# Attention probabilities transposed on VectorE in 32x32 squares, with the squares exchanged through DRAM, in a two-layer diffusion backbone

## The chip, the cores and the metric

The kernel runs on one core of one Trainium2 chip. The metric is the device time of one execution in microseconds, lower is better. Four engines do the work: TensorE (PE in the profile, with its weight loads as PEld), VectorE (DVE), ScalarE (ACT) and GpSimd (POOL). SyncE (SP) issues nearly all DMAs; ACT issues the few of the rotary swap.

## The reference

Two layers work on a latent stream of 1024 tokens with 1024 channels. The first is windowed attention with 16 query heads over 4 key/value heads of 128 channels, the second a gated convolution module. Only the attention is touched. Each block of 128 queries sees its own block of keys, the block before, the block after and 256 context keys, in one softmax with a learned sink:

```
s_win = einsum('bqhgd,bkhd->bhgqk', qblk, kw) * scale
s_win = where(mask, s_win, -inf)
s_ctx = einsum('bqhgd,bchd->bhgqc', qblk, kc) * scale
p_ctx, p_win = sink_softmax(sink_l, s_ctx, s_win)
o = einsum('bhgqc,bchd->bqhgd', p_ctx, vc) + einsum('bhgqk,bkhd->bqhgd', p_win, vw)
```

`y = (o * silu(z)) @ w_out`, and the layer adds `gate * y` to its input. The scores leave TensorE with queries on the partitions; the product with the values wants the probabilities with keys on the partitions. So every block of probabilities, 128 queries by 512 or 640 keys, must be transposed.

## The kernel before, in words

Each f32 operand is split into a high and a low part, and a product is three matmuls (high by high, high by low, low by high). The kernel has a first part (modulation, the projections of the first heads), the attention, the output projection, and the convolution layer.

The attention is a loop over 128 steps (line 1280): 16 heads, and in each head 8 blocks of 128 queries. I write a step as (head, block). TensorE's instructions stand in the order of the program; those of the other engines are put in order by a scheduler that works ahead of the run. What step (h, b) puts on TensorE, in this order:

- `scores` (line 1083) of the **next** step: six matmuls into one of two PSUM buffers `pss`. Behind them on the other engines: DVE adds the mask and takes the maximum (`p_page<-pss`, here "the reduce"), ACT takes the exponential and its sum, DVE the reciprocal, POOL scales by it ("the scale"). The result is `p_page`.
- `fill(12)` (line 1070): twelve matmuls of the q and z projections of the next head, into `psg`.
- `pv` (line 1153) if it is due. `pv(h, half)` multiplies four blocks of probabilities by values and context values: 18 matmuls that read `pthi` and `ptlo`. It is put into a queue behind block 3 or 7 and so stands in the step after that. `pv(5, 0)` stands in step (5, 4), `pv(5, 1)` in step (6, 0). I call the stretch between two `pv` a half. Behind every second head `pv_shared` does the two edges between the halves.
- `transposes` (line 1119) of the step's own block: 4 or 5 transposes of 128x128 on TensorE into a `pss` buffer, then ACT copies them to `pthi` (the high part, "hi"), and DVE subtracts to get `ptlo` ("lo").

At the end of every fourth head there is a longer step ("regroup", line 1308), in which the whole k and v projections of the next group run on TensorE.

`pthi` and `ptlo` have 22 places of 128 columns. The places of a block are used again by the block four steps later, so hi of (h, 4) can't be written until `pv(h, 0)` has read them.

Beside this, DVE does one step of a long sum per loop step (`ada_rest`, line 665: "ada" below, 0.48 us each, its input loaded by SP one step ahead); it is held behind the lo of the softmax (`after`, line 660). `low_parts` (line 724) makes the low parts of the output weights on ACT ("lhi") and POOL, and SP stores them. SBUF is handed out as 45 pages of 4 KB per partition in turn.

Of the kernel before, what the change touches and what calls it, by code (L numbers as in the profile page):

```python
# [14 lines left out]
P = 128  # L15
# [15 lines left out]
TB = T // P  # L31
# [63 lines left out]
def backbone_kernel(  # L95
# [987 lines left out]
    def scores(h, qb):  # L1083
        g = h // 4
        q = qt[h]
        kk = kvt[g]
        c = kk[2]
        k0, k1 = max(qb - 1, 0), min(qb + 1, TB - 1)
        nw = (k1 - k0 + 1) * P
        s = ps_s()  # L1090
        w0 = 512 - nw
        qsl = slice(qb * P, qb * P + P)
        ksl = slice(k0 * P, k0 * P + nw)
        for n, (a, b) in enumerate(((0, 0), (0, 1), (1, 0))):
            PE.matmul(s[:, w0:512], q[a][:, qsl], kk[b][:, ksl], start=n == 0, stop=n == 2)
            PE.matmul(s[:, 512:768], q[a][:, qsl], c[:, b], start=n == 0, stop=n == 2)
        p = pg.alloc(F32, [1024], "p")
        sc8 = small([P, 3], name="sc", bufs=6)
        nmx, l0, ri = (sc8[:, i:i + 1] for i in range(3))
        w = nw + CT  # L1100

        act(p[:, w:w + 1], nsink[:, h:h + 1], AF.Copy)
        sc = dict(scale=-SCALE, scalar=nsink[:, h:h + 1], op0=ALU.add, op1=ALU.min, accum_out=nmx)
        if qb == TB - 1:
            V.tensor_tensor_reduce(
                out=p[:, 0:w].rearrange("p (a b) -> p a b", a=2),
                in0=s[:, w0:768].rearrange("p (a b) -> p a b", a=2),
                in1=mask.rearrange("p (a b) -> p a b", a=2)[:, :, 0:256],
                **sc)
        else:  # L1110
            V.tensor_tensor_reduce(out=p[:, 0:w], in0=s[:, w0:768], in1=mask[:, 640 - w:640], **sc)
        act(p[:, 0:w + 1], p[:, 0:w + 1], AF.Exp, bias=nmx, scale=-1.0, accum_out=l0)
        V.reciprocal(ri, l0)
        anchor_p[:] = [G.tensor_scalar(out=p[:, 0:w], in0=p[:, 0:w], scalar1=ri, scalar2=1.0, op0=ALU.mult, op1=ALU.mult)]
        ptile[(h, qb)] = p
        if qb == TB - 1:
            pg.free(*qt.pop(h))

    def transposes(h, qb):
        p = ptile.pop((h, qb))  # L1120
        k0, k1 = max(qb - 1, 0), min(qb + 1, TB - 1)
        nb = k1 - k0 + 1
        tb = ps_s()
        ql = qb % 4
        for kb in range(k1, k0 - 1, -1):
            at = 2 - 2 * (kb - qb)
            PE.transpose(tb[:, at * P:(at + 1) * P], p[:, (kb - k0) * P:(kb - k0 + 1) * P], ident)
        for i in range(2):
            at = 1 + 2 * i
            PE.transpose(tb[:, at * P:(at + 1) * P], p[:, (nb + i) * P:(nb + i + 1) * P], ident)  # L1130
        pg.free(p)
        tv = tb[:, 0:640].rearrange("p (a b) -> p a b", b=P)
        a0, a1 = int(qb == TB - 1), 4 if qb == 0 else 5
        runs = [(a0, a1, slice(ql + 4 * a0, ql + 4 * a1 - 3, 4))]
        if h % 2 == 0 and qb == 3:
            runs = [(1, 5, slice(7, 20, 4)), (0, 1, slice(20, 21))]
        elif h % 2 == 0 and qb == 4:
            runs = [(0, 4, slice(0, 13, 4)), (4, 5, slice(21, 22))]
        for r0, r1, bs in runs:
            anchor_a[:] = [act(pthi[:, bs], tv[:, r0:r1], AF.Copy)]  # L1140
        for r0, r1, bs in runs:
            anchor[:] = [split_lo(V, ptlo[:, bs], tv[:, r0:r1], pthi[:, bs])]

    shared = []

    def pv_mm(o, work):
        for n, (a, b, ps_, os_) in enumerate(work):
            last = n == len(work) - 1
            PE.matmul(o[:, os_], a, pthi[:, ps_], start=n == 0, stop=False)
            PE.matmul(o[:, os_], a, ptlo[:, ps_], start=False, stop=False)  # L1150
            PE.matmul(o[:, os_], b, pthi[:, ps_], start=False, stop=last)

    def pv(h, half):
        if half == 2:
            return pv_shared(h)
        c, vh, vl = kvt[h // 4][2:5]
        o = ps_o(0)
        q0 = half * 4
        work = [(*(c[:, n, i * P:i * P + P] for n in (2, 3)), slice(4 + 8 * i, 8 + 8 * i), slice(0, 512)) for i in range(2)]
        for kb in range(q0, q0 + 4):  # L1160
            qa, qz = max(kb - 1, q0), min(kb + 1, q0 + 3)
            b0 = qa - q0 + 8 * (qa - kb + 1)
            work.append((vh[:, kb], vl[:, kb], slice(b0, b0 + 9 * (qz - qa) + 1, 9), slice((qa - q0) * P, (qz - q0 + 1) * P)))
        pv_mm(o, work)
        sl = slice(half * 512, half * 512 + 512)
        if h % 2 == 0 and half == 0:
            shared[:] = [pg.alloc(F32, [1024], "ozs")]
        part = shared[0]
        oz = hp.alloc(F32, None, "oz")
        own, edge = (slice(128, 512), slice(0, 128)) if half else (slice(0, 384), slice(384, 512))  # L1170
        zv = zt[h][:, sl]
        e0 = 256 * half + 128 * (1 - h % 2)
        stt(oz[:, 0:512], o, 0.5, zv, ALU.mult, ALU.mult)
        V.tensor_copy(part[:, e0:e0 + 128], oz[:, edge])
        SY.dma_start(out=ozd[h, :, sl][:, own], in_=oz[:, own])
        hp.free(oz)
        if half:
            act(part[:, 768 - 256 * (h % 2):1024 - 256 * (h % 2)], zt[h][:, 384:640], AF.Copy)
            pg.free(zt.pop(h))

    def pv_shared(h):

        vh, vl = kvt[h // 4][3:5]

        o = ps_o(0)
        pv_mm(o[:, 0:256], [(vh[:, 4], vl[:, 4], slice(3, 21, 17), slice(0, 256))])
        pv_mm(o[:, 256:512], [(vh[:, 3], vl[:, 3], slice(16, 22, 5), slice(0, 256))])
        part = shared.pop()
        oz = hp.alloc(F32, None, "oz")
        ov, sv, pv_ = (t[:, 0:512].rearrange("p (q e n) -> p e q n", q=2, e=2) for t in (o, oz, part))  # L1190
        zv = part[:, 512:1024].rearrange("p (e q n) -> p e q n", q=2, e=2)
        for e in range(2):
            stt(sv[:, e], ov[:, e], 0.5, zv[:, e], ALU.mult, ALU.mult)
        tt(V, oz[:, 0:512], oz[:, 0:512], part[:, 0:512], ALU.add)
        for e in range(2):
            SY.dma_start(out=ozd[h - e, :, 384:640].rearrange("p (q n) -> p q n", q=2), in_=sv[:, e])
        hp.free(oz)
        pg.free(part)
        if h % 4 == 3:
            pg.free(vh, vl)  # L1200
# [79 lines left out]
    for i, (h, qb) in enumerate(steps):  # L1280
        if qb == 0:
            for n in (() if h % 4 == 3 else (h + 1,) if h % 4 or not h else (h, h + 1)):
                enqueue(("z", n))
                if n + 1 < NH:
                    enqueue(("q", n + 1))
        if (h, qb) == (NH - 1, EARLY_FROM - 2):
            run(lows)
        if h == NH - 1 and EARLY_FROM - 2 <= qb < EARLY_FROM:
            next(projA)
        if (h, qb) == (NH - 1, EARLY_FROM):  # L1290
            next(projA)
            fillq.append((("wo", 0), early_proj()))
        nxt = steps[i + 1] if i + 1 < len(steps) else None
        regroup = nxt and nxt[1] == 0 and nxt[0] % 4 == 0
        if nxt and nxt[1] == 0:
            fill(1000, ("q", h + 1))
        if nxt and not regroup:
            scores(*nxt)
        if not regroup:
            n = 15 if h and h % 4 == 0 and qb < 4 else FILL  # L1300
            if h // 4 in vlate and h:
                fill(3)
                n -= 3
                vlate.pop(h // 4)()
            fill(n)
        if pvq:
            pv(*pvq.popleft())
        if regroup:
            g = nxt[0] // 4
            old = kvt[g - 1]  # L1310
            run(job(("k", g)))
            transposes(h, qb)
            run(job(("v", g)))
            pv(h, 1)
            pg.free(*old[:3])
            scores(*nxt)
            continue
        transposes(h, qb)
        if lstate[0] == "open" or h and (h % 4 < 3 or qb < LOWS):
            lstate[0] = next(lows, "shut")  # L1320
        else:
            store()
        if qb % 4 == 3:
            pvq.append((h, qb // 4))
        if qb == 1 and h and h % 2 == 0:
            pvq.append((h - 1, 2))
        for _ in range(2 if qb == 1 or qb == 6 and h % 2 else 1):
            if next(adag, None):
                break
# [646 lines left out]
```

## Time and profile before

| | |
|---|---|
| runs of the kernel before | 1686.21, 1686.81, 1686.99 us; median 1686.81 |
| span of the profiled execution | 1684.8 us, first to last instruction |
| outside the span | 2.0 us, median less span (the profiled execution's own whole time isn't listed) |
| PE busy | 1675.0 us, 99% |
| DVE, ACT, POOL busy | 1116.1, 878.8, 871.0 us |
| DMA | 244.55 MB, 145 GB/s over the span |
| granted TensorE clock | 0.999 |

The attention loop lies between about 75 and 805 us. A busy time says in how much of the span an instruction of that engine was under way. Matmuls overlap, so the pace of TensorE is read from the starts of its instructions, not from their durations. The order in which instructions stand on DVE and SP decides what waits behind what, since each engine runs its own list in order.

### The profile page before, as it was taken

The page shows a single profiled execution, that of the slowest core. Times are in us where ns is not written, and L with a number is a line of the kernel's source. Part 1 is how long each engine was busy: PE and PEld are TensorE (multiplying, and loading weights), DVE is VectorE, ACT ScalarE, POOL GpSimd, SP SyncE. Part 2 cuts the span into 40 slices and gives each one's busy share as a digit, 9 for nine tenths or more (in the row PEclk, how much of TensorE's full clock was granted, in tenths as well). Part 3 has the DMA queues.
Part 4 walks back from the last instruction along what each step waited for, and adds up shares of the span by engine and source line. Part 5 has one row for each costly group of instructions (what it writes and reads, how often), then busy time and mean ns, then how long its engine had stood idle before and what let it go on. Part 6 is the DMA issues. An engine that isn't in the chain of part 4 may idle for free.

```text
span 1684.8 us, 23963 instructions
## 1 busy us (share of the span) xinstructions
PE 1675.0 (99%) x8436; PEld 1413.9 (84%) x8436; DVE 1116.1 (66%) x2131; ACT 878.8 (52%) x1555; POOL 871.0 (52%) x722
## 2 busy tenths in 40 slices
PE   9999999999999999999999999999999999999998
PEld 6888888888888888888888888888888888888886
DVE  5765654566356644566324289999999999868732
ACT  5745543555355543556334365555665654566741
POOL 0256653666366663653001267999898888130400
PEclk9999999999999999999999999999999999999999
DMA  9424443454244443447976522020211202387881
GB/s 387 150 85 153 134 121 95 153 153 141 84 152 144 143 135 98 135 135 251 320 233 228 213 94 91 11 72 17 75 51 51 82 33 80 130 276 241 310 298 50
DMA packets 114776, 244.55 MB, mean 145 GB/s; under 512 B 11626, under 2 KB 36514, under 8 KB 114656
## 3 DMA queue, kind: packets, MB, share of 16 engines
q1 hardware_dynamic: 108576, 233.06, 40.9%
q10 hardware_dynamic: 6080, 9.97, 2.4%
q8 instruction: 66, 1.08, 0.3%
q14 instruction: 54, 0.44, 0.1%
HBM read 190.80 MB, written 41.69 MB: 138 GB/s over the span
## 4 chain that ended last, share of the span: by engine, by line
PE 98%; DVE 0%; DMA 0%; ACT 0%; POOL 0%; issue 0%; ACTq 0%; POOLq 0%
PE psg L89 51%; PE pss L89 26%; PE pso L89 22%; DMA rope_half<-rope_half 0%; POOL rope_half L89 0%; DVE x_page L89 0%; ACT p_page L89 0%; DVE wlo_page L89 0%; ACT pthi L89 0%; ACT rope_half L89 0%; ACT whi_page L89 0%; DVE hf_page L89 0%; DVE hl_page L89 0%; ACT qh_page L89 0%; ACT lhi_page L89 0%
## 5 line engine op out<-in xcount | busy, mean ns | idle before, releaser
L89 POOL TENSOR_TENSOR odd_half<-odd_half,prod_half 128x513 f32<-128x513 f32 (+2 forms) x252 | 314.7, 1257 | 22.6 <-ACT prod_half L89 9.4
L89 POOL TENSOR_TENSOR wlo_page<-wraw_page,whi_page 128x512 fp32r<-128x512 f32 (+1 forms) x104 | 173.0, 1680 | 186.7 <-DVE ql_page L89 72.0
L89 PE MATMUL psg<-hh_page,whi_page 128*128 128x512 f32 x600 | 236.3, 394 | 0.0
L89 PE MATMUL psg<-hl_page,whi_page 128*128 128x512 f32 x600 | 234.4, 391 | 0.0
L89 PE MATMUL psg<-hh_page,wlo_page 128*128 128x512 f32 x600 | 234.0, 390 | 0.0
L89 ACT ACTIVATE prod_half<-ubuf,dww 128x513 f32<-128x513 f32 (+2 forms) x252 | 165.6, 675 | 116.9 <-POOL odd_half L89 113.0
L89 PE MATMUL psg<-h2h_page,whi_page 128*128 128x512 f32 x464 | 181.9, 392 | 0.0
L89 PE MATMUL psg<-h2h_page,wlo_page 128*128 128x512 f32 x464 | 180.6, 389 | 0.0
L89 PE MATMUL psg<-h2l_page,whi_page 128*128 128x512 f32 x464 | 180.6, 389 | 0.0
L89 POOL TENSOR_SCALAR p_page<-p_page,sc 128x640 f32<-128x640 f32 (+1 forms) x128 | 99.6, 779 | 149.5 <-DVE sc L89 131.8
L89 DVE SCALAR_TENSOR_TENSOR pss<-ubuf,dww,pss 128x512 f32<-128x512 f32 (+3 forms) x270 | 172.4, 670 | 0.1
L89 DVE SCALAR_TENSOR_TENSOR pss<-ubuf,wsum,pss 128x512 f32<-128x512 f32 (+3 forms) x270 | 171.7, 671 | 0.2
L89 ACT ACTIVATE p_page<-p_page,sc 128x641 f32<-128x641 f32 (+1 forms) x128 | 102.9, 804 | 98.3 <-DVE sc L89 95.9
L89 ACT ACTIVATE pthi<-pss 128x512 fp32r<-128x512 f32 (+2 forms) x144 | 87.3, 618 | 109.7 <-PE pss L89 99.8
L89 DVE TENSOR_TENSOR ptlo<-pss,pthi 128x512 fp32r<-128x512 f32 (+2 forms) x144 | 101.8, 716 | 61.2 <-ACT pthi L89 59.9
L89 PEld LDWEIGHTS psg<-hh_page,wlo_page 128*128 128x128 f32 x600 | 112.7, 188 | 24.3
L89 PEld LDWEIGHTS psg<-hh_page,whi_page 128*128 128x128 f32 x600 | 112.8, 188 | 19.2 <-ACT hh_page L89 0.3
L89 PEld LDWEIGHTS psg<-hl_page,whi_page 128*128 128x128 f32 x600 | 112.8, 188 | 18.4
L89 ACT ACTIVATE whi_page<-wraw_page 128x1024 fp32r<-128x1024 f32 x88 | 92.6, 1052 | 49.8 <-PE psg L89 21.1
L89 PE MATMUL pso<-h2h_page,whi_page 128*128 128x512 f32 x304 | 118.3, 389 | 0.0
L89 PE MATMUL pso<-h2h_page,wlo_page 128*128 128x512 f32 x304 | 118.3, 389 | 0.0
L89 PE MATMUL pso<-h2l_page,whi_page 128*128 128x512 f32 x304 | 118.3, 389 | 0.0
(262 smaller groups left out, 3992.4 us busy)
## 6 DMA issues: line engine op xcount, KB each, us to landing
wraw_page<-in_k_wconv_dram SPq DMA_DIRECT2D x48, 512.0 KB, 3.3
wraw_page<-in_k_win_dram SPq DMA_DIRECT2D x40, 512.0 KB, 3.6
wo_page<-in_attn_w_out_dram SPq DMA_DIRECT2D x32, 512.0 KB, 6.2
wol_page<-wolA SPq DMA_DIRECT2D x32, 512.0 KB, 8.3
wo_page<-in_conv_w_out_dram SPq DMA_DIRECT2D x32, 512.0 KB, 6.7
wol_page<-wolC SPq DMA_DIRECT2D x32, 512.0 KB, 6.2
rope_half<-rope_half ACTq DMA_DIRECT2D x76, 128.0 KB, 2.4
araw_page<-in_k_ada_dram SPq DMA_DIRECT2D x16, 512.0 KB, 10.1
```

The lines of the kernel that those rows point to most:

```text
L89: r = f(*a, **k)
```

## The change

The four or five transposes on TensorE go. In `scores`, behind the scale, DVE now transposes the block in squares of 32x32 into a new page (`psq_page`, below "T"): within each strip of 32 partitions the squares are turned, but a square stays in its strip. SP stores that page to one of four DRAM buffers (`squares`). `land`, at the start of the block's own step, issues four loads on SP, one for each strip of 32 partitions, which fetch the squares that belong there into another page (`pt_page`). `split_p` then makes hi on ACT and lo on DVE from that page in SBUF, where before both read PSUM. The order of the places in `pthi` and `ptlo` changes with it, and `pv_mm` takes them as access patterns made by hand; the matmuls are the same in number and size.

```diff
@@ scores
-        ptile[(h, qb)] = p
+        nt = w // P
+        sq = pg.alloc(F32, [1024], "psq")
+        V.transpose(out=sq[:, 0:w].rearrange("p (b t j) -> p t b j", b=4, t=nt),
+                    in_=p[:, 0:w].rearrange("p (t b j) -> p t b j", t=nt, b=4))
+        pg.free(p)
+        z = squares[(h * TB + qb) % len(squares)]
+        SY.dma_start(out=z[:, 0:w], in_=sq[:, 0:w])
+        pg.free(sq)
...
-    def transposes(h, qb):
+    squares = [dr.tile([P, 640], F32, tag=f"psq{i}", name=f"psq{i}") for i in range(4)]
+
+    def land(h, qb):
+
+        nt = 4 if qb in (0, TB - 1) else 5
+        z = squares[(h * TB + qb) % len(squares)]
+        p = ptile[(h, qb)] = pg.alloc(F32, [1024], "pt")
+        for b in range(4):
+            SY.dma_start(out=p[32 * b:32 * b + 32, 0:nt * P].rearrange("p (a x) -> p a x", a=4),
+                         in_=z[:, b * nt * 32:(b + 1) * nt * 32].rearrange("(a p) x -> p a x", p=32))
...
+    def split_p(h, qb):
...
-            PE.transpose(tb[:, at * P:(at + 1) * P], p[:, (kb - k0) * P:(kb - k0 + 1) * P], ident)
...
-            PE.transpose(tb[:, at * P:(at + 1) * P], p[:, (nb + i) * P:(nb + i + 1) * P], ident)
+        pv_ = p[:, 0:nt * P].rearrange("p (a t j) -> p t a j", a=4, t=nt)
...
-            anchor_a[:] = [act(pthi[:, bs], tv[:, r0:r1], AF.Copy)]
+            anchor_a[:] = [act(slots(pthi, b0, r1 - r0), pv_[:, r0:r1], AF.Copy)]
...
-            anchor[:] = [split_lo(V, ptlo[:, bs], tv[:, r0:r1], pthi[:, bs])]
+            anchor[:] = [split_lo(V, slots(ptlo, b0, r1 - r0), pv_[:, r0:r1], slots(pthi, b0, r1 - r0))]
...
@@ the loop over steps
+        land(h, qb)
         if nxt and not regroup:
             scores(*nxt)
...
-        transposes(h, qb)
+        split_p(h, qb)
```

How this stands on DVE in head 5, at blocks 4 to 6. Before, the rows from the reciprocal of block (5, 5) on; `ptlo_76<-pss_248` is lo of (5, 4), `ptlo_76<-pss_252` lo of (5, 5), and the `ISA` row is the reduce of (5, 6):

```order
L89 RECIPROCAL sc_246_3382<-sc_246_3382 128x1
L89 TENSOR_TENSOR rope_half_75_3458<-psg_243_3349,cos_page_78_560 128x512
L89 SCALAR_TENSOR_TENSOR oz_half_72_3419<-pso_247_3400,zs_page_226_3156 128x512
L89 COPY ozs_page_218_3012<-oz_half_72_3419 128x128
L89 TENSOR_TENSOR ptlo_76<-pss_248_3423,pthi_75 128x5x128
L89 ISA p_page_239_3442,sc_250_3443<-pss_249_3435,mask_page_82_597,nsink_72 128x640
L89 ISA sc_250_3443 128x1
L89 RECIPROCAL sc_250_3443<-sc_250_3443 128x1
L89 COPY mod1_604<-pso_69_945 128x2
L89 TENSOR_TENSOR ptlo_76<-pss_252_3480,pthi_75 128x5x128
```

Now, the same place; `pt_page_321`, `326` and `330` are blocks (5, 3), (5, 4) and (5, 5), `psq_page_328` is T of (5, 5), and `oz_half_72` reads the result of `pv(5, 0)`:

```order
L89 TENSOR_TENSOR ptlo_76<-pt_page_321_3451,pthi_75 128x5x128
L89 SCALAR_TENSOR_TENSOR pso_69_952<-wsum_raw_606,cs_131,pso_69_952 128x256
L89 STREAM_TRANSPOSE psq_page_328_3515<-p_page_327_3508 128x5x4x32
L89 COPY mask_page_82_597<-pso_69_952 128x256
L89 TENSOR_TENSOR ptlo_76<-pt_page_326_3496,pthi_75 128x5x128
L89 SCALAR_TENSOR_TENSOR oz_half_72_3549<-pso_203_3530,zs_page_307_3272 128x512
L89 ISA p_page_331_3571,sc_205_3572<-pss_204_3564,mask_page_82_597,nsink_72 128x640
L89 ISA sc_205_3572 128x1
L89 COPY ozs_page_293_3122<-oz_half_72_3549 128x128
L89 TENSOR_TENSOR ptlo_76<-pt_page_330_3559,pthi_75 128x5x128
L89 COPY mod1_604<-pso_69_952 128x2
L89 RECIPROCAL sc_205_3572<-sc_205_3572 128x1
```

What moved: lo of (5, 3), which stood ahead of the rows shown, now stands ahead of T of (5, 5). Lo of (5, 5) now stands ahead of the reciprocal of (5, 6), so the softmax of (5, 6) can't go on until (5, 5) has come back from DRAM.

The same place on SP. Before:

```order
L89 DMA dww_raw_605<-in_ada_w_dram 128x256
L89 DMA wsum_raw_606<-in_ada_w_dram 128x256
L89 DMA wolA_607<-low_page_232_3286 128x1024
L89 DMA wraw_page_242_3454<-in_k_win_dram 128x1024
L89 DMA ozd_601<-oz_half_72_3419 128x384
L89 DMA low_page_246_3583<-in_attn_w_out_dram 128x2x512
```

Now; a row `psq..` is the store of a block, `pt_page.. x4` its four loads, for blocks (5, 3), (5, 4) and (5, 5):

```order
L89 DMA psq3_613<-psq_page_320_3430 128x640
L89 DMA dww_raw_605<-in_ada_w_dram 128x256
L89 DMA psq0_610<-psq_page_323_3470 128x640
L89 DMA pt_page_321_3451<-psq3_613 32x4x160 x4
L89 DMA pt_page_326_3496<-psq0_610 32x4x160 x4
L89 DMA wsum_raw_606<-in_ada_w_dram 128x256
L89 DMA psq1_611<-psq_page_328_3515 128x640
L89 DMA wolA_607<-low_page_317_3404 128x1024
L89 DMA pt_page_330_3559<-psq1_611 32x4x160 x4
```

What moved: SP has five more DMAs for each step, and the loads of (5, 3) stand behind the store of (5, 4), which waits for that block's T.

More of the change, by code (lines that the diff above doesn't have):

```diff
@@ L1116, in scores @@
+        pg.free(sq)
         if qb == TB - 1:
             pg.free(*qt.pop(h))
-    def transposes(h, qb):
-        p = ptile.pop((h, qb))
[L1121 to L1126, printed above, removed]
-            PE.transpose(tb[:, at * P:(at + 1) * P], p[:, (kb - k0) * P:(kb - k0 + 1) * P], ident)
-        for i in range(2):
-            at = 1 + 2 * i
-            PE.transpose(tb[:, at * P:(at + 1) * P], p[:, (nb + i) * P:(nb + i + 1) * P], ident)
-        pg.free(p)
[L1132 to L1139, printed above, removed]
-            anchor_a[:] = [act(pthi[:, bs], tv[:, r0:r1], AF.Copy)]
-        for r0, r1, bs in runs:
-            anchor[:] = [split_lo(V, ptlo[:, bs], tv[:, r0:r1], pthi[:, bs])]
@@ new lines, in backbone_kernel, with slots @@
+    squares = [dr.tile([P, 640], F32, tag=f"psq{i}", name=f"psq{i}") for i in range(4)]
[6 more added lines that the diff above has]
+                         in_=z[:, b * nt * 32:(b + 1) * nt * 32].rearrange("(a p) x -> p a x", p=32))
+    def slots(t, b0, n):
+        return t[:, b0:b0 + 4 * n - 3:4].rearrange("p t (a j) -> p t a j", a=4)
@@ new lines, in split_p @@
+    def split_p(h, qb):
+        p = ptile.pop((h, qb))
+        ql, a0 = qb % 4, int(qb == 0)
+        nt = 4 if qb in (0, TB - 1) else 5
+        pv_ = p[:, 0:nt * P].rearrange("p (a t j) -> p t a j", a=4, t=nt)
+        if qb == 0:
+            runs = [(0, 4, 4)]
+        elif qb == TB - 1:
+            runs = [(0, 2, ql), (2, 4, ql + 12)]
+        elif h % 2 == 0 and qb == 3:
+            runs = [(0, 2, ql), (3, 5, ql + 12), (2, 3, 20)]
+        elif h % 2 == 0 and qb == 4:
+            runs = [(1, 5, ql + 4), (0, 1, 21)]
+        else:
+            runs = [(0, 5, ql)]
+        for r0, r1, b0 in runs:
+            anchor_a[:] = [act(slots(pthi, b0, r1 - r0), pv_[:, r0:r1], AF.Copy)]
+        for r0, r1, b0 in runs:
+            anchor[:] = [split_lo(V, slots(ptlo, b0, r1 - r0), pv_[:, r0:r1], slots(pthi, b0, r1 - r0))]
+        pg.free(p)
@@ L1144, in backbone_kernel, with pthi_lo @@
     shared = []
+    def pthi_lo(b0, step, n):
+        return [bass.AP(t.tensor, t.offset + b0 * P, [t.ap[0], (step * P, n), (1, P)])
+                for t in (pthi[:, 0:22].rearrange("p b n -> p (b n)"), ptlo[:, 0:22].rearrange("p b n -> p (b n)"))]
     def pv_mm(o, work):
@@ L1148, in pv_mm @@
             last = n == len(work) - 1
-            PE.matmul(o[:, os_], a, pthi[:, ps_], start=n == 0, stop=False)
-            PE.matmul(o[:, os_], a, ptlo[:, ps_], start=False, stop=False)
-            PE.matmul(o[:, os_], b, pthi[:, ps_], start=False, stop=last)
+            ph, pl = ps_
+            PE.matmul(o[:, os_], a, ph, start=n == 0, stop=False)
+            PE.matmul(o[:, os_], a, pl, start=False, stop=False)
+            PE.matmul(o[:, os_], b, ph, start=False, stop=last)
     def pv(h, half):
@@ L1158, in pv @@
         q0 = half * 4
-        work = [(*(c[:, n, i * P:i * P + P] for n in (2, 3)), slice(4 + 8 * i, 8 + 8 * i), slice(0, 512)) for i in range(2)]
+        work = [(*(c[:, n, i * P:i * P + P] for n in (2, 3)), pthi_lo(12 + 4 * i, 1, 4), slice(0, 512)) for i in range(2)]
         for kb in range(q0, q0 + 4):
             qa, qz = max(kb - 1, q0), min(kb + 1, q0 + 3)
-            b0 = qa - q0 + 8 * (qa - kb + 1)
-            work.append((vh[:, kb], vl[:, kb], slice(b0, b0 + 9 * (qz - qa) + 1, 9), slice((qa - q0) * P, (qz - q0 + 1) * P)))
+            work.append((vh[:, kb], vl[:, kb], pthi_lo(qa - q0 + 4 * (kb - qa + 1), -3, qz - qa + 1),
+                         slice((qa - q0) * P, (qz - q0 + 1) * P)))
         pv_mm(o, work)
@@ L1185, in pv_shared @@
         o = ps_o(0)
[L1186 to L1187 removed]
+        pv_mm(o[:, 0:256], [(vh[:, 4], vl[:, 4], pthi_lo(11, 9, 2), slice(0, 256))])
+        pv_mm(o[:, 256:512], [(vh[:, 3], vl[:, 3], pthi_lo(0, 21, 2), slice(0, 256))])
         part = shared.pop()
@@ L1317, in backbone_kernel @@
             continue
-        transposes(h, qb)
+        split_p(h, qb)
         if lstate[0] == "open" or h and (h % 4 < 3 or qb < LOWS):
```

## The prediction

> **What bounds the kernel now.** I read the page's busy times first, then its chain of work that ended last.
>
> ```profile
> PE 1675.0 (99%) x8436; PEld 1413.9 (84%) x8436; DVE 1116.1 (66%) x2131; ACT 878.8 (52%) x1555; POOL 871.0 (52%) x722
> PE 98%; DVE 0%; DMA 0%; ACT 0%; POOL 0%; issue 0%; ACTq 0%; POOLq 0%
> ```
>
> TensorE is the bound throughout, and the chain lies on it. Next the attention loop: TensorE's timeline over a step and a `pv`, and the starts of the DVE instruction behind each `pv`.
>
> ```profile
> 403.01 0.39 PE L89 MATMUL psg<-hh_page,wlo_page 128*128 128x512 f32 x1
> 403.24 0.71 PE L89 MATMUL pss<-ident,p_page 128*128 128x128 f32 x5
> 403.70 0.42 PE L89 MATMUL pss<-kh_page,qh_page 128*128 128x384 f32 x1
> 404.67 0.40 PE L89 MATMUL psg<-hh_page,whi_page 128*128 128x512 f32 x1
> 407.40 0.40 PE L89 MATMUL pso<-pthi,kvc_page 128*128 128x512 f32 x1
> 410.56 0.71 PE L89 MATMUL pss<-ident,p_page 128*128 128x128 f32 x5
> 411.10 0.50 PE L89 MATMUL pso<-ones,mask_page 128*128 128x1 f32 x4
> ...
> 371.22 0.69 DVE L89 SCALAR_TENSOR_TENSOR oz_half<-pso,zs_page 128x512 f32<-128x512 f32 x1 [1.83 <-PE pso L89]
> 391.06 0.69 DVE L89 SCALAR_TENSOR_TENSOR oz_half<-pso,zs_page 128x512 f32<-128x512 f32 x1 [1.84 <-PE pso L89]
> 410.76 0.69 DVE L89 SCALAR_TENSOR_TENSOR oz_half<-pso,zs_page 128x512 f32<-128x512 f32 x1 [1.77 <-PE pso L89]
> ```
>
> From starts: scores take 0.97 us (403.70 to 404.67), twelve fill matmuls 2.73 (to 407.40), a `pv` 3.16 (to 410.56), five transposes 0.46 and 0.54. A half lasts 19.8 us (371.22 to 391.06, 391.06 to 410.76). DVE waits for `pv`, never the other way round.
>
> **What is removed.** 608 transposes, by this row 87.2 us of busy time:
>
> ```profile
> L89 PE MATMUL pss<-ident,p_page 128*128 128x128 f32 x608 | 87.2, 272 | 0.1
> ```
>
> Durations of overlapping matmuls overstate it. By starts a transpose holds TensorE for 0.50 / 5 = 0.10 us: 608 x 0.10 = 61 us, 2.0 us a half. If nothing else became late, that would be the gain. `pv` reads the same number of columns, so I leave it as it is.
>
> **What is added.** Per step one T on DVE, one store and four loads on SP. DVE has room: in this stretch of the windows view it is busy 110.14 of 200 us (third pair of numbers; POOL is the fifth, the DMA share the last but one).
>
> ```profile
> 400.00:600.00 200.00, 200.00 (x1122) 175.82 (x1120) 110.14 (x246) 99.89 (x214) 115.03 (x104) 1.00 0.43 133
> ```
>
> So throughput isn't the question; the way there and back is. Before, a block went from POOL through TensorE to ACT in one hop. Now it goes POOL, DVE, SP, DRAM, SP, ACT, DVE, and DVE's list has a block's lo ahead of the next block's reciprocal: DVE stands still, and the next softmax with it, until the block is back. Prices, from the groups of instructions between 69 and 810 us, the DMA issues, and one SP issue:
>
> ```profile
> L89 DVE CUSTOM_DVE_ANT_0 p_page<-pss,mask_page,nsink 128x640 f32<-128x640 f32 x96 | 84.1, 876 | 3.9 <-PE pss L89 3.5
> L89 DVE TENSOR_TENSOR ptlo<-pss,pthi 128x640 fp32r<-128x640 f32 x80 | 65.6, 820 | 28.5 <-ACT pthi L89 28.0
> L89 DVE SCALAR_TENSOR_TENSOR pso<-wsum_raw,cs,pso 128x256 f32<-128x256 f32 x64 | 30.7, 480 | 0.6 <-DMA wsum_raw<-in_ada_w_dram 0.4
> L89 DVE TENSOR_TENSOR rope_half<-psg,cos_page 128x512 f32<-128x512 f32 x36 | 24.8, 690 | 23.1 <-ACT rope_half L89 22.0 <-ACT p_page L89 0.8
> L89 DVE SCALAR_TENSOR_TENSOR zs_page<-zs_page,psg 128x512 f32<-128x512 f32 x32 | 21.9, 684 | 9.3 <-ACT zs_page L89 9.3
> L89 DVE RECIPROCAL sc<-sc 128x1 f32<-128x1 f32 x128 | 20.8, 162 | 76.7 <-ACT p_page L89 75.8
> L89 DVE COPY ozs_page<-oz_half 128x128 f32<-128x128 f32 x32 | 16.5, 516 | 1.2
> L89 DVE CAST woh_page<-wo_page 128x1024 fp32r<-128x1024 f32 x1 | 0.7, 740 | 0.0
> ...
> L89 ACT ACTIVATE p_page<-p_page,sc 128x641 f32<-128x641 f32 x96 | 79.7, 831 | 84.4 <-DVE sc L89 82.0 <-DMA low_page<-in_attn_w_out_dram 0.5 <-ACT rope_half L89 0.5
> L89 ACT ACTIVATE pthi<-pss 128x640 fp32r<-128x640 f32 x80 | 56.1, 701 | 46.8 <-PE pss L89 45.9 <-PE pso L89 0.6
> L89 ACT ACTIVATE lhi_page<-low_page 128x512 fp32r<-128x512 f32 x64 | 40.1, 626 | 0.0
> L89 ACT ACTIVATION_READ_ACCUMULATOR p_page<-p_page,sc 128x1 f32 x128 | 23.9, 187 | 0.0
> ...
> L89 POOL TENSOR_SCALAR p_page<-p_page,sc 128x640 f32<-128x640 f32 x96 | 77.4, 806 | 128.0 <-DVE sc L89 110.8 <-PE pss L89 10.4 <-PE pso L89 3.0
> ...
> dww_raw<-in_ada_w_dram SPq DMA_DIRECT2D x64, 128.0 KB, 2.9
> rope_half<-rope_half ACTq DMA_DIRECT2D x76, 128.0 KB, 2.4
> wolC<-low_page SPq DMA_DIRECT2D x16, 512.0 KB, 3.0
> ozd<-oz_half SPq DMA_DIRECT2D x32, 192.0 KB, 1.9
> ...
> 411.34 0.33 SPq L89 DMA_DIRECT2D wraw_page<-in_k_win_dram  x1
> ```
>
> The reduce is 0.88 (with its accumulator read about 0.96), the exponential 0.83 + 0.19, the reciprocal 0.16, the scale 0.81, hi 0.70, lo 0.82, ada 0.48, 0.35 us an issue on SP, 0.1 a hand-over between engines. Instructions on 512 columns I take at four fifths. No row shows T. Below lies the cast, 1024 columns in 0.74, so 640 in 0.46; above I allow twice the lo, 1.7. I take 0.85, the reduce and the lo being the nearest. The store (320 KB) lies between 1.9 (192 KB) and 3.0 (512 KB): 2.4. A load (80 KB, 32 partitions) lies between 1.9 and 2.9, and I take the rotary swap's 2.4. The trip from the end of T to the end of lo is then 0.1 + 2.4 + 0.1 + three issues 1.05 + 2.4 + 0.1 + 0.70 + 0.1 + 0.82 = 7.8 us, beside a step of five.
>
> **One half, walked.** Zero is the end of T(5, 4); the lists are those shown with the change. SP issues the store of (5, 4) and only then the loads of (5, 3): the last lands at 1.5 + 2.4 = 3.9, hi ends 4.7, lo 5.6; `pv(5, 0)` runs 5.7 to 8.9. Behind lo DVE does ada and T(5, 5), to 6.95. Hi of (5, 4) must wait until `pv(5, 0)` has read its places: 9.0 to 9.7; lo to 10.6, oz to 11.3, the reduce of (5, 6) to 12.25. Then lo of (5, 5): stored 7.05 to 9.45, landed 13.0, hi 13.8, lo 14.7. The exponential of (5, 6) stands on ACT behind that hi and lhi, so it ends 15.45, the reciprocal 15.7. Two ada (0.48, 0.35), the reduce of (5, 7), one ada (0.35): T(5, 6) ends 18.6, T(5, 7) behind its scale 20.3. Rope and the reduces of (6, 0) and (6, 1) take DVE to 22.8, while (5, 6) is away: stored 21.1, landed 24.65, hi 25.45, lo 26.4. Two ada, a reciprocal, T(6, 0) to 28.2, zs 28.9, lo of (5, 7) 29.6. `pv(5, 1)` starts at 29.7. From `pv` to `pv`: 24.0 us, two trips of nearly 8 and the softmax legs between them. TensorE has 3.2 + 4 x 0.97 + 4 x 2.73 = 18.0 us of work in it and waits the other 6, ahead of `pv`.
>
> The half before it and the two behind it, walked with the same prices along the same lists, give 26.5, 25.4 and 25.0; the mean of the four is 25.2, which is 5.4 above 19.8.
>
> **A second cost on DVE.** Lo has read PSUM and SBUF; now both its inputs are in SBUF. The same subtraction or sum with two SBUF inputs, and a copy in SBUF, show what that can mean beside POOL:
>
> ```profile
> L89 DVE TENSOR_TENSOR rope_half<-rope_half,rope_half 128x512 f32<-128x512 f32 x9 | 9.4, 1047 | 14.0 <-POOL rope_half L89 14.0
> L89 DVE TENSOR_TENSOR oz_half<-oz_half,ozs_page 128x512 f32<-128x512 f32 x7 | 4.8, 689 | 0.1
> ...
> L89 DVE COPY ozs_page<-oz_half x32: 221/229/1342, 103.9 to 808.4; 128x128 f32<-128x128 f32 x32
> ```
>
> The copy takes 0.23 at the median and up to 1.34, on average 0.29 more than the median; one sum takes 0.36 more than the other. I add 0.3 for each of the two lo on the path of a half. The Trainium skill, "SBUF — State Buffer", section "Who interferes with whom", has VectorE with two SBUF inputs and GpSimd reading SBUF take one lock for a whole instruction, the later one blocked. These rows agree with it; by the rule, with POOL busy 115 of 200 us and its long instructions about 1.3 us, my estimate would be 0.37 a lo, 4 us more in all.
>
> **The sum.** Of 32 halves three have the regroup, whose projections cover the trips, and the last has the output projection's first rows: they gain 2.0 each, -8. The other 28 lose 5.4 each, +151, and the lo 28 x 2 x 0.3 = +17. Span 1684.8 + 160 = 1845; the runs' median is 2.0 above the span, so 1847 us. Low end: DMAs at 1.9 and T at 0.46 shorten a half by 2 x 1.0 + 3 x 0.4 = 3.2 to 22.0: 28 x 2.2 - 8 = +54, 1741. High end: 3.0, 2.9 and 1.7 lengthen it by 2.2 + 2.5 to 29.9: 28 x 10.1 - 8 + 17 = +292, 1979.
>
> **Rivals.** *The trip is hidden* (other side, faster). For it: DVE and SP have room, and the block has two steps until its `pv`. Against it: the order on DVE, which ties each softmax to the block before. It decides where a half falls under 19.8, so if each of the two trips takes 2.7 us less, 5.1 instead of 7.8. At best nothing waits: 1686.8 - 61 = 1626. Chance 0.08. *Break-even* within 0.2% (about what a measurement of this kernel can tell from none): 0.03.
>
> *TensorE also runs slower behind each wait.* The first matmuls of the kernel show it:
>
> ```profile
> 1.98 2.08 PE L89 MATMUL pss<-zerr_page 128*128 128x512 f32 x4 [1.98 <-DVE zerr_page L89]
> 4.26 8.69 PE L89 MATMUL pss<-zerr_page 128*128 128x512 f32 x28
> ```
>
> In the fill a 512-column matmul starts every 0.23 us (2.73 / 12). At that pace the four would take 1.1 us and the 28 behind them 6.6; they take 2.08 and 8.69, 3.1 more together. The granted clock reads 1.00 there all the same. If each wait of 6 us costs such a slow start, and half of it lies on the path (behind the other half DVE is late anyway), it is 28 x 3.1 / 2 = 43 more: 1890. For it: the waits are long. Against: no wait in this trace is, so nothing shows that a wait does it. Chance 0.18. The Trainium skill, "TensorE: Matmul & The Clock Gate", section "HAM oscillation — how this bites in real kernels", has it that an idle gap over about 3.4 us puts the array back to half clock; the start of this trace agrees, and no later wait in it can show it.
>
> That the transposes stay can't be: they are gone from TensorE's list.
>
> **How the numbers follow.** The forecast has 0.70, the clock 0.18, hidden 0.08, break-even 0.03, slower by less than the low end 0.01. The range 1740 to 1970 holds the walk's bounds and the clock; some 0.1 lies below and 0.08 above. Faster 0.08, same 0.03, slower 0.89.
>
> **What would show it.** TensorE idle ahead of `pso<-pthi` some 28 x 6 = 170 us in all, released by DVE `ptlo`; DVE waiting for ACT `pthi`, and ACT for the DMAs into `pt_page`; halves near 25 us between the `oz_half` starts; T near 0.85; a store near 2.4. Wrong if halves are under 20, if TensorE waits elsewhere (for `pss`, say), or if a trip measures under 5.1 us.

## The result and the profile after

The changed kernel takes 1935.81 us, median of 4 runs (1931.32 to 1937.86); the kernel before, on the same chip, 1686.51 (1685.15 to 1686.99). The ratio is 1.148, 95% interval 1.146 to 1.149: slower by 249 us. The profiled execution spans 1935.4 us against 1684.8, so 250.6 us are to be found in the traces. The page's busy times and its chain of work that ended last:

```profile
PE 1691.5 (87%) x7828; PEld 1403.8 (73%) x7828; DVE 1246.9 (64%) x2283; ACT 892.1 (46%) x1579; POOL 890.6 (46%) x722
PE 50%; DMA 10%; DVE 4%; issue 2%; SPq 2%; ACT 2%; POOL 1%; ACTq 0%; DVEq 0%; POOLq 0%
```

TensorE had 99% of the span and 98% of the chain; now it has 87% and 50%, and the chain passes through DMA, DVE and queues. TensorE has 608 instructions fewer (8436 to 7828) and yet is busy 16.5 us longer: it runs slower. The windows view of the same stretch as before has its granted clock at 0.88 where it was 1.00:

```profile
400.00:600.00 200.00, 151.43 (x719) 128.27 (x719) 108.24 (x206) 74.62 (x161) 91.33 (x77) 0.88 0.57 173
```

The waits of TensorE alone (total, times, longest):

```profile
PE pso L89 <- ACT pthi L89: 163.0, 26, 9.6
PE psg L89 <- ACT ozh_page L89: 23.1, 2, 13.6
PE pso L89 <- DVE ptlo L89: 18.0, 19, 3.0
```

163.0 + 18.0 = 181 us of waiting stand ahead of `pso`, that is ahead of `pv`; all rows of this view together make 236.1 us, against 2.2 before. Who made `pv` wait, from the waits of all engines:

```profile
ACT pthi L89 <- DMA pt_page<-psq: 191.6, 86, 12.0
DVE ptlo L89 <- ACT pthi L89: 164.0, 88, 13.8
ACT p_page L89 <- DMA psq<-psq_page: 64.0, 24, 7.7
DVE p_page L89 <- DMA psq<-psq_page: 48.3, 15, 7.9
```

The first two rows are the trip: hi waits for the loads, lo for hi. The last two were not in my list. A softmax wants a page of SBUF for its `p`. The kernel's list gives out the page that was freed longest ago, and that can be one which a turned block has left; the softmax may write only when the store of that block has landed. ACT (which writes the sink's column first) and DVE (the reduce) stand still for that, 112 us together. The prices, first by groups of instructions:

```profile
L89 DVE STREAM_TRANSPOSE psq_page<-p_page 128x640 f32<-128x640 f32 x96 | 80.6, 841 | 34.4 <-POOL p_page L89 32.7 <-DMA psq<-psq_page 1.4
L89 DVE TENSOR_TENSOR ptlo<-pt_page,pthi 128x640 fp32r<-128x640 f32 x80 | 78.0, 975 | 104.0 <-ACT pthi L89 100.3 <-DMA pt_page<-psq 2.8 <-DMA gd<-mask_page 0.6
L89 PE MATMUL pso<-pthi,kvc_page 128*128 128x512 f32 x128 | 69.6, 591 | 163.0 <-ACT pthi L89 163.0
```

Then the DMA issues (KB each, median us from issue to landing):

```profile
psq<-psq_page SPq DMA_DIRECT2D x96, 320.0 KB, 3.5
pt_page<-psq SPq DMA_DIRECT2D x384, 80.0 KB, 2.4
rope_half<-rope_half ACTq DMA_DIRECT2D x76, 128.0 KB, 4.4
```

T takes 0.841 us, lo 0.975 (it took 0.820), the store 3.5, a load 2.4. The rotary swap, which nobody touched, lands after 4.4 us where it took 2.4. The last row of the groups is a matmul of `pv`: 591 ns, where the same work took 396 before:

```profile
L89 PE MATMUL pso<-pthi,kvc_page 128*128 128x512 f32 x128 | 45.5, 396 | 0.0
```

The timeline of the `pv` that ends near 411 shows how this goes together (start, duration; DVE and its `oz_half` starts first, then SP, ACT, TensorE):

```profile
351.17 0.69 DVE L89 SCALAR_TENSOR_TENSOR oz_half<-pso,zs_page 128x512 f32<-128x512 f32 x1 [0.20 <-PE pso L89]
381.07 0.68 DVE L89 SCALAR_TENSOR_TENSOR oz_half<-pso,zs_page 128x512 f32<-128x512 f32 x1
387.74 0.84 DVE L89 STREAM_TRANSPOSE psq_page<-p_page 128x640 f32<-128x640 f32 x1 [0.93 <-POOL p_page L89]
395.98 0.83 DVE L89 TENSOR_TENSOR ptlo<-pt_page,pthi 128x640 fp32r<-128x640 f32 x1 [0.19 <-ACT pthi L89]
402.63 0.88 DVE L89 CUSTOM_DVE_ANT_0 p_page<-pss,mask_page,nsink 128x640 f32<-128x640 f32 x1 [4.11 <-DMA psq<-psq_page]
411.42 0.68 DVE L89 SCALAR_TENSOR_TENSOR oz_half<-pso,zs_page 128x512 f32<-128x512 f32 x1
...
388.62 0.33 SPq L89 DMA_DIRECT2D psq<-psq_page  x1
391.80 1.75 SPq L89 DMA_DIRECT2D pt_page<-psq  x4
397.98 0.32 SPq L89 DMA_DIRECT2D psq<-psq_page  x1
...
402.83 0.20 ACT L89 ACTIVATE p_page<-nsink 128x1 f32<-128x1 f32 x1 [5.48 <-DMA psq<-psq_page]
...
405.22 0.79 PE L89 MATMUL pso<-pthi,kvc_page 128*128 128x512 f32 x1 [8.50 <-ACT pthi L89]
406.42 0.80 PE L89 MATMUL pso<-ptlo,kvc_page 128*128 128x512 f32 x1 [0.41 <-DVE ptlo L89]
407.87 0.63 PE L89 MATMUL pso<-ptlo,kvc_page 128*128 128x512 f32 x1
408.30 0.63 PE L89 MATMUL pso<-pthi,kvc_page 128*128 128x512 f32 x1
```

Three things are to be seen. One trip: T ends at 387.74 + 0.84 = 388.58, its store is issued at 388.62, the loads from 391.80, lo ends at 395.98 + 0.83 = 396.81; that is 8.2 us. Then the page: the next reduce starts only at 402.63, held 4.11 us by a store (ACT is held 5.48 by the same), and behind that softmax on ACT stands the hi that `pv` needs; TensorE has been idle 8.50 us when it starts at 405.22. Then the pace: from 407.87 to 408.30 are 0.43 us a matmul of 512 columns, where the fill before takes 0.23. The two halves between the `oz_half` starts last 29.9 and 30.35 us; before, 19.8. They are among the longer ones: of the 31 stretches between the 32 such starts, the 25 that lasted under 24 us before have gone from 19.9 to 28.9 us on the mean.

A balance on TensorE itself: +250.6 in the span = 236.1 - 2.2 = +233.9 of waiting, minus what the transposes held, plus the slower pace. Experiment no_turn gives the transposes as 58 us (below), so 250.6 - 233.9 + 58 = 75 us are slower pace. The busy times say the same: no_turn has the change's 7828 matmuls and is busy 1616.7 us with them, the change 1691.5.

### The profile page after: what moved, and what is told of

The parts are those of the page before. It is cut to its first block, busy times and chain, and to the rows that moved or that the text cites. A ratio compares the mean times of both kernels' runs of the same rounds, so it can differ in the third digit from the quotient of the medians.

```text
span 1935.4 us, 24249 instructions
## 1 busy us (share of the span) xinstructions
PE 1691.5 (87%) x7828; PEld 1403.8 (73%) x7828; DVE 1246.9 (64%) x2283; ACT 892.1 (46%) x1579; POOL 890.6 (46%) x722
## 2 busy tenths in 40 slices
DMA packets 206944, 324.30 MB, mean 168 GB/s; under 512 B 21866, under 2 KB 112290, under 8 KB 206816
## 4 chain that ended last, share of the span: by engine, by line
PE 50%; DMA 10%; DVE 4%; issue 2%; SPq 2%; ACT 2%; POOL 1%; ACTq 0%; DVEq 0%; POOLq 0%
PE psg L89 24%; PE pso L89 14%; PE pss L89 12%; DMA psq<-psq_page 5%; DMA pt_page<-psq 4%; SPq L89 2%; DVE ptlo L89 1%; ACT pthi L89 1%; DMA rope_half<-rope_half 1%; DVE psq_page L89 1%; DVE p_page L89 1%; DMA wolC<-low_page 1%; POOL wlo_page L89 0%; POOL p_page L89 0%; DVE pso L89 0%
## 5 line engine op out<-in xcount | busy, mean ns | idle before, releaser
L89 DVE TENSOR_TENSOR ptlo<-pt_page,pthi 128x640 fp32r<-128x640 f32 (+3 forms) x168 | 142.1, 861 | 172.3 <-ACT pthi L89 164.0
L89 PE MATMUL pso<-pthi,kvc_page 128*128 128x512 f32 x128 | 69.6, 591 | 163.0 <-ACT pthi L89 163.0
L89 ACT ACTIVATE pthi<-pt_page 128x640 fp32r<-128x640 f32 (+3 forms) x168 | 94.9, 585 | 231.7 <-DMA pt_page<-psq 191.6
L89 PEld LDWEIGHTS pso<-pthi,kvc_page 128*128 128x128 f32 x128 | 35.8, 280 | 179.8 <-ACT pthi L89 174.0
L89 DVE STREAM_TRANSPOSE psq_page<-p_page 128x640 f32<-128x640 f32 (+1 forms) x128 | 103.2, 807 | 48.8 <-POOL p_page L89 46.9
L89 POOL TENSOR_TENSOR rope_half<-rope_half,sin_page 128x512 f32<-128x512 f32 x38 | 49.3, 1297 | 184.4 <-DMA rope_half<-rope_half 170.2
L89 DVE CUSTOM_DVE_ANT_0 p_page<-pss,mask_page,nsink 128x640 f32<-128x640 f32 (+1 forms) x112 | 95.5, 857 | 56.8 <-DMA psq<-psq_page 42.3
```

Source lines behind the costliest of these rows:

```text
L89: r = f(*a, **k)
```

## The experiments

All were timed against the kernel before on the same chip (1686 to 1687 us).

| kernel | us | ratio (95%) |
|---|---|---|
| no_turn | 1644.9 | 0.9754 (0.9726 to 0.9782) |
| no_exchange | 1689.3 | 1.0017 (1.0006 to 1.0027) |
| store_only | 1711.8 | 1.0143 (1.0122 to 1.0163) |
| turn_only | 1717.2 | 1.0183 (1.0153 to 1.0212) |
| dma_only | 1789.0 | 1.0609 (1.0578 to 1.0639) |
| dma_p | 1791.7 | 1.0625 (1.0594 to 1.0656) |
| dma_one | 1815.7 | 1.0761 (1.0743 to 1.0780) |
| cut | 1838.3 | 1.0896 (1.0872 to 1.0919) |
| traffic | 1865.3 | 1.1062 (1.1040 to 1.1084) |
| late | 1872.5 | 1.1123 (1.1072 to 1.1175) |
| one_load | 1922.3 | 1.1389 (1.1364 to 1.1414) |
| the change | 1935.8 | 1.1478 (1.1461 to 1.1494) |
| warm | 1968.3 | 1.1673 (1.1649 to 1.1696) |

My theory at the start was the prediction's: the trip's length, met by each `pv`, is the whole loss, and T, issues and bytes find room. The first rival: the added traffic costs by itself, whoever waits for it. The second: DVE's time for T costs by itself.

**no_exchange**: the changed kernel with T, without store and loads; hi and lo read the page that T wrote, so the squares stay in their strips of partitions.

```
-        z = squares[...]
-        SY.dma_start(out=z[:, 0:w], in_=sq[:, 0:w])
-        pg.free(sq)
+        ptile[(h, qb)] = sq
...
-        land(h, qb)
```

> T stays on VectorE, but the store and the four loads are left out: hi and lo are made from the page that T wrote, so squares are not exchanged between strips. My theory (the way through DRAM is what the softmax waits for): the halves fall back to TensorE's own work, 18 us, so about 1626 to 1645 us. Rival (T and the lo from SBUF load VectorE and its port beside GpSimd too heavily): it stays above 1800.

Measured 1689.3 us: no trip at all, and still nothing of the transposes' 61 us is gained. My theory lost its first part here; the rival's 1800 isn't reached either. The windows view and TensorE's waits of this run:

```profile
400.00:600.00 200.00, 187.57 (x947) 161.79 (x946) 139.16 (x282) 99.94 (x216) 118.77 (x101) 0.97 0.42 130
```

```profile
PE pss L89 <- POOL ql_page L89: 15.4, 9, 3.3
PE pss L89 <- ACT qh_page L89: 6.1, 2, 3.4
```

DVE is busy 139.16 of 200 us, far from full, but TensorE waits a little in 29 places, 47.2 us over all rows. The two greatest are for the queries, whose rotary part passes through DVE on its way to ACT and POOL. The next run, without T, has 19.4 us of waits, so T makes this work late although DVE is not saturated.

**no_turn**: the same without T as well; hi and lo read the scaled `p`, which is not transposed at all.

```
-        V.transpose(out=sq..., in_=p...)
+        ptile[(h, qb)] = p
...
-        land(h, qb)
```

> The changed kernel without T and without the exchange: hi and lo are made straight from the scaled page, so nothing is transposed at all. Theory of before (each transpose holds TensorE 0.10 us): 1626 to 1640 us, and what lies between this and 1689 is the price of T on VectorE. Rival (TensorE doesn't become free, since reading the probabilities from SBUF or two score buffers cost as much): 1670 or more.

Measured 1644.9, just above the first case: the transposes' removal alone brings 42 us. The span is 41.0 us shorter while TensorE's waits are 19.4 us instead of 2.2, so the transposes had held TensorE for 41.0 + 17.2 = 58 us. From no_turn to no_exchange, T on DVE costs 1689.3 - 1644.9 = 44 us.

**turn_only**: the kernel before, with T written to a page that nobody reads, and no DMA.

```
+        V.transpose(out=sq..., in_=p...)
+        pg.free(sq)
```

> The kernel before with T added, its result read by nobody, no DMA. If VectorE's room (55% busy) takes the 0.84 us a step: 1687 to 1700. If T in VectorE's list delays the softmax of the next step: 1710 or more, and then a good part of the 178 us of the run with T, store and loads is T's.

Measured 1717.2, +30 us, as in the second case: T costs in the other surroundings too.

**traffic**: the kernel before, its transposes kept on TensorE, plus T, the store and the four loads (into a page that is freed at once), all unread.

```
+        V.transpose(out=sq..., in_=p...)
+        SY.dma_start(out=z[:, 0:w], in_=sq[:, 0:w])
+        pg.free(sq)
...
+        land(h, qb)
```

> The kernel before, with its transposes on TensorE, and T, the store and the four loads added, whose result nobody reads. My theory (it is the wait, not the traffic): within 1% of before, 1687 to 1700 us. Rival (the 84 MB more and the small packets, or five more DMAs a step on the SP queue, slow everything): 1750 or more.

Measured 1865.3, +179 us, with nothing of the block waiting for its trip (the bytes added are 80 MB, not 84: 324.30 in the changed kernel against 244.55). The rival's bound holds. That is the second part of my theory gone: the additions have a price of their own. Two of its waits:

```profile
DVE psq_page L89 <- DMA pt_page<-psq: 44.7, 20, 4.0
PE pss L89 <- DVE ptlo L89: 45.3, 21, 4.6
```

The first row is again a page that may not be written until a transfer has landed, here the loads into the freed page.

**dma_only** and **dma_p**: the kernel before with store and loads only; the loads fill one page kept for that (44 are left for the rest). In dma_only the store reads the constant mask page and so waits for nothing; in dma_p it reads the block's `p` (`in_=p[:, 0:w]`).

```
+        SY.dma_start(out=z[:, 0:w], in_=mask[:, 0:w])
...
+        p = own
...
+        land(h, qb)
```

> The kernel before with a store (from the constant mask page) and the four loads of each step, into one page of their own, read by nobody; the other pages are 44. No wait for a computed result, no page held: traffic and issue alone. If the traffic or the number of DMAs on SP is what costs: 1780 to 1870. If the 178 us come from what waits (SP waiting for T, pages that are free only after a store): 1687 to 1705.

> As the run before, but the store takes the scaled page p itself: SP now waits in its list for the softmax of each step, and p's page is not free until the store has landed. If waiting on SP and held pages are the cause: 1750 or more, well above the run with the mask page. If not, the two are within 1%.

Measured 1789.0 and 1791.7: +102 and +105 us. The transfers of the two lie differently in time, as the rows of the store show, dma_only's first (duration min/median/max, first and last start):

```profile
L89 SPq DMA_DIRECT2D psq<-mask_page x128: 319/432/1565, 54.0 to 605.3; - x128
```

```profile
L89 SPq DMA_DIRECT2D psq<-p_page x128: 319/421/1592, 81.3 to 894.1; - x128
```

The two are within 1%, so by the second case of dma_p a store that waits for its block and holds its page costs nothing of its own. But the runs differ in more than that: a store that waits for nothing ran ahead of its block (to 605 us), the one of `p` kept step (to 894), as in the change. dma_p is therefore the nearer to the change. What its traffic made late, from its waits (SP's own, then all engines'):

```profile
SPq L89 <- DMA psq<-p_page: 171.7, 101, 4.8
...
DVE pso L89 <- DMA wsum_raw<-in_ada_w_dram: 34.9, 14, 5.0
DVE pso L89 <- DMA dww_raw<-in_ada_w_dram: 26.1, 16, 4.0
POOL rope_half L89 <- DMA rope_half<-rope_half: 74.7, 23, 6.5
```

SP issues in order, and ahead of each block's loads it stands until the store has landed: 101 times, 171.7 us. The loads queued behind come late, and DVE stands 61 us for the two of ada, against 0.4 + 2.1 us in the kernel before. In the change, though, the same two rows are 3.8 + 4.7 us: what is late in dma_p isn't what is late there. The swap, on ACT's queue, isn't behind SP and is late too (55.5 us of POOL's waiting before). How the 105 us divide between SP's standing still and crowded transfers no run separates; a second queue for the exchange wasn't tried.

**dma_one** and **store_only**: dma_only with one load of 128 partitions in place of four, and dma_only without loads.

```
-        for b in range(4):
-            SY.dma_start(out=p[32 * b:32 * b + 32, ...], in_=z[...])
+        SY.dma_start(out=p[:, 0:nt * P], in_=z[:, 0:nt * P])
```

> dma_only (the kernel before with the added traffic, unread) with one straight load in place of the four. Small packets and issues as the cause: 1690 to 1725, against 1789.0 for dma_only. Bytes as the cause: 1770 or more.

> dma_only without its loads: the kernel before plus only the 320 KB store a block. If the loads are what costs, 1687 to 1705; if bytes cost alike in both directions, half of the 102 us: about 1738; if the store itself is the dear part, over 1765.

Measured 1815.7, in the case for bytes, and 1711.8, between the first two cases. One straight load isn't cheaper; the run with it is 27 us slower than dma_only. Both ran ahead of their blocks even further, dma_one's store first:

```profile
L89 SPq DMA_DIRECT2D psq<-mask_page x128: 320/432/1639, 54.7 to 534.3; - x128
```

```profile
L89 SPq DMA_DIRECT2D psq<-mask_page x128: 319/448/2040, 54.0 to 231.2; - x128
```

In dma_one all the traffic lies before 550 us, in store_only before 235; they compare pilings of transfers as much as kinds. SP also stood until the one page of the loads was filled, 270.2 us in dma_one and 92.5 in dma_only, a wait that only these kernels have. So the two runs don't settle whether small packets are the cause, and how the price divides between store and loads stays open.

**one_load**: the same edit in the changed kernel, where the store keeps step. The squares are turned but not exchanged between strips.

> The changed kernel with one load of 128 partitions (2560 B to a row, straight) in place of the four that pick the squares in rows of 640 B; squares are turned but not exchanged between partitions. Bytes, the store and the wait for the trip stay. If the four small loads (their issues on SP and their 640 B packets) are what makes the traffic dear, most of the 102 us of dma_only goes: 1830 to 1860. If the bytes or the trip's length are, it stays above 1905; between these, both.

Measured 1922.3, 13.5 us under the change, with intervals that don't touch. The four small loads, their issues and their rows of 640 B, account for some 14 of 249 us; as the second case had it, they are not the main cause.

**cut**: the changed kernel with its store and loads, but hi and lo read T's page in place; the loaded page goes back unread. The squares are not exchanged.

```
-        pg.free(sq)
+        ptile[(h, qb)] = sq
...
-        p = ptile[(h, qb)] = pg.alloc(F32, [1024], "pt")
+        p = pg.alloc(F32, [1024], "pt")
...
+        pg.free(p)
```

> The changed kernel with its store and its four loads as they are, but hi and lo read the turned page in place; the page that the loads fill goes back unread, so squares are not exchanged. Only the wait of the split for the trip is cut, the traffic stays. If waiting for the trip makes most of what the exchange costs beyond the traffic's 102 us: 1780 to 1810. If the traffic with its queueing, and pages held until transfers land, make it: 1850 to 1930.

Measured 1838.3, between the two cases. Against the change, waiting for the trip is worth 1935.8 - 1838.3 = 98 us; against no_exchange, the exchange that nobody waits for costs 1838.3 - 1689.3 = 149. The edit also changes how long pages are held: T's page is kept for hi and lo, and the loaded one is given back at once. Its waits, TensorE's two greatest and those for pages:

```profile
PE psg L89 <- POOL wlo_page L89: 43.7, 11, 10.7
PE pso L89 <- ACT pthi L89: 24.7, 12, 9.3
...
DVE psq_page L89 <- DMA pt_page<-psq: 67.2, 23, 6.1
DVE p_page L89 <- DMA pt_page<-psq: 27.4, 14, 4.1
ACT p_page L89 <- DMA pt_page<-psq: 27.1, 16, 4.6
```

The wait ahead of `pv` falls from 163.0 to 24.7 us, as it should where nothing waits for the trip. The page waits remain, 122 us on DVE and ACT. How the 149 us divide isn't shown. With dma_p's 105 for the traffic, 44 would be left, and traffic leaves the same by its own sum, 179 - 30 (turn_only) - 105; I put these 44 to pages held until a transfer lands. But dma_p is another burden: DVE's waits for ada's loads, 61 us there, are 11 here, and dma_p holds pages itself. And TensorE's greatest wait here, 43.7 us, is for weights that POOL makes, not for a softmax. No run changes the number of pages alone.

**late**: the changed kernel with landing, split and `pv` of each block one step later, so that a trip has one step more.

```
-        land(h, qb)
+        if i and not behind:
+            land(*steps[i - 1])
...
-        split_p(h, qb)
+        if i and not behind:
+            split_p(*steps[i - 1])
...
-        if qb % 4 == 3:
-            pvq.append((h, qb // 4))
+        if qb == 4:
+            pvq.append((h, 0))
+        if qb == 0 and h % 4:
+            pvq.append((h - 1, 1))
...
```

In the three long steps of the regroup two blocks are split in the same step, so there the last block has no step more.

> The changed kernel with land, split_p and pv one step later each, the same instructions. My theory (a trip of about 8 us against one step of slack): with a second step of slack TensorE finds its operands ready; 1630 to 1690 us, halves of 18 to 20 us. Rival (throughput of VectorE, of the DMA queue, or the pages, which are no more than before): it stays above 1850.

Measured 1872.5: 63 us better than the change, and 186 worse than before.

```profile
PE pso L89 <- ACT pthi L89: 88.7, 23, 8.6
...
ACT p_page L89 <- DMA psq<-psq_page: 42.1, 17, 7.2
DVE p_page L89 <- DMA psq<-psq_page: 40.6, 17, 6.4
```

A step more brings the waits ahead of `pv` from 163.0 + 18.0 to 88.7 + 19.8 us and doesn't end them: the page waits go on, and with them softmaxes that are late. My theory, which had the kernel under 1690 here, is refuted in this form; the rival's bound holds.

**warm**: the changed kernel with 20 matmuls ahead of each `pv`, whose results `pv` overwrites.

```
+        for _ in range(20):
+            PE.matmul(o, vh[:, 0], kvt[h // 4][0][:, 0:512], start=True, stop=True)
```

> The changed kernel with 20 more matmuls of 512 columns ahead of each pv (4.6 us at full pace, in time in which TensorE waits anyway), their result overwritten. If the slow start behind each wait costs time on the path, the time falls although there is more work: some 40 us less than the changed kernel, about 1895. If VectorE is late anyway, no change: 1925 to 1945. If the waits are shorter than I think, the added work costs: 1960 and more.

Measured 1968.3, 32 us slower than the change and in the last case, though the mean granted clock rises from 0.929 to 0.965 and the wait shrinks:

```profile
PE pso L89 <- ACT pthi L89: 75.5, 22, 6.9
```

All of TensorE's waits fall from 236.1 to 146.1 us, but it is busy 1812.2 us instead of 1691.5: filled in this way, the gaps cost 121 us of work and give back 90 of waiting. The waits themselves were as long as thought (163.0 us in 26). The run doesn't say what a fast start alone would give, since the 20 matmuls also push back `pv` wherever the wait was shorter than they are.

**The loss, put together**: before 1686.5; transposes gone -42 (no_turn); T on DVE +44 (no_exchange); the exchange that nobody waits for +149 (cut); waiting for the trip +98 (the change against cut). The sum is +249, as it must be, since each term is the step from one kernel of a chain to the next. From no_turn on all have the same 7828 matmuls, so where TensorE is busy longer, its pace is slower, and the profiles divide each step:

| kernel | waits of TensorE, us | TensorE busy, us | mean granted clock |
|---|---|---|---|
| no_turn | 19.4 | 1616.7 | 0.995 |
| no_exchange | 47.2 | 1630.5 | 0.988 |
| cut | 158.8 | 1673.9 | 0.954 |
| the change | 236.1 | 1691.5 | 0.929 |

In these profiled executions T adds 28 us of waits and 14 of slower pace, the exchange that nobody waits for 112 and 43, the trip 77 and 18. So the 75 us of slower pace come in with each step that adds waits, and most of them not with the trip.

## Why the prediction was right or wrong

**Direction and place: right.** Slower, with TensorE idle ahead of `pv`: 170 us were foretold there and 181 stand there. That this fits is luck in part: the prediction's own halves of 25.2 us, with 18.0 of work in each, make 28 x 7.2 = 202. Another 55 us of waits stand elsewhere, most of them ahead of `psg` and `pss`, which it named as a sign of being wrong. The releaser shown for most is ACT's `pthi`, not DVE's `ptlo`, because `pv` begins with hi. The chain foretold (DVE for hi, ACT for the loads) is the two greatest new rows.

**Prices.** T 0.85 foretold, 0.841 measured; load 2.4, 2.4; the trip 7.8, 8.2 in the one shown. The store, 2.4, took 3.5, above its neighbours (1.9 to 3.0). Why isn't shown: the window moves 173 GB/s where it moved 133, but in traffic and late, with 190 and 189, the same store takes 2.8 and 2.7. Lo's 0.3 beside POOL was 0.975 - 0.820 = 0.16, in no_turn 1.069 - 0.820 = 0.25.

**Removal: right for TensorE, wrong for the time.** 61 us were foretold, 58 were held. Only 42 came out, because other engines, hidden until then, are late next (17 us of waits in no_turn). The halves with a regroup were to gain 2.0 us each and gained nothing: the six long stretches around the regroups went from 34.4 to 40.2 us on the mean.

**The step that failed: "So throughput isn't the question; the way there and back is."** I read DVE's 110 of 200 us and SP's free time as room. no_exchange shows T eating the whole gain with DVE at 139 of 200, and dma_p shows the traffic costing 105 us with nobody waiting for its data. 149 us of the exchange are not the trip's dependency; 98 are. The waits' total came out nearly right (below) while the greater part of their cause was another one; that the time lies so near is luck. The halves were given 25.2 us; the ordinary ones last 28.9 on the mean.

**What the walk left out.** The page that a softmax gets: the walk followed instructions and queues, and not who frees the buffer. In the changed kernel 112 us of ACT's and DVE's waiting are for that.

**The rivals.** *TensorE also slower* had 0.18 and is most of what the sum lacks. On TensorE the forecast's +160 meant 160 + 61 = 221 us of waits; 234 were found. Of the 250.6 - 160 = 91 us missing, 13 are waits, 3 the transposes (58 for 61), and 75 the slower pace, which the rival had at 43. Its ground against, that no wait in the trace of before is long, spoke of the wrong kernel, since the forecast itself put waits of 6 us there. That the time would fall by 75 with a fast start isn't shown; warm, which got part of the clock back, got no time back. *Hidden* was wrong even with the trip taken away: no_exchange is at 1.0017.

## What to carry to other kernels

An engine at 55% and a queue with gaps are not free: ask what stands behind the new instruction in its list, price the added work alone, with its result unread, before looking at latency; then see whether the same waits stand in the real kernel. For a buffer that is handed to a DMA, count it as taken until the transfer has landed, and look for who gets it next. Where a forecast puts new waits on the bound engine, its pace behind a wait belongs into the sum.

## What the runs showed of the hardware

- After 8.50 us without work TensorE's matmuls of 512 columns start every 0.43 us instead of 0.23, for some 3.7 us (405.22 to about 408.9); the windows view has the granted clock at 0.53 from 398 to 409 us and at 1.00 from 409 to 420. The Trainium skill, "TensorE: Matmul & The Clock Gate", section "HAM oscillation — how this bites in real kernels", has an idle gap over about 3.4 us bring half clock: this wait agrees.
- In the change the swap of 128 KB lands after 4.4 us at the median instead of 2.4, though its own queue carries nothing more. The added bytes alone don't make that: it lands after 2.8 us in warm, with the same DMAs and the same DMA share of 0.57 in the window, and after 3.0 in no_turn, which adds none.
- On DVE, T of fp32 squares costs 0.841 us for 128x640, as much as a subtraction of that size (0.820). That subtraction takes 0.975 us in the change and 1.069 in no_turn; in both its two inputs lie in SBUF, where before one lay in PSUM.
